# Moving squares, products and state scans between four engines in layer 0 of a two-layer streaming encoder

## The chip, the cores and the metric

The kernel runs on one core of a Trainium2 chip. The core has five engines that follow instruction streams of their own: TensorE (PE in the profile, with its weight loads as PEld), VectorE (DVE), ScalarE (ACT), GpSimd (POOL) and SyncE (SP, which here issues the transfers). They meet at semaphores only: an instruction that waits holds up all that stands behind it on its engine. The metric is the device time of one execution in microseconds, lower is better.

## What is computed

Two groups of frames, 1024 of a prompt and 8 x 16 of running streams, 1152 columns in all, go through two trunk layers with the same weights. Layer 0, in which the change lies, cut to what matters:

```python
h = rmsnorm(x, norm_mix[0])                       # x * rsqrt(mean(x*x)) * w
proj = h @ w_in                                   # 1024 -> S5 input u, q, k, v, z, b, a
# mixer A: S5, 32 groups of 16 channels, a complex state of 64 for each
lam_bar = exp(lam * dt)
b_bar = ((lam_bar - 1) / lam)[..., None] * b      # operators, from the weights alone
x_t = lam_bar * x_{t-1} + b_bar @ u_t             # a scan along time
y_t = real(c @ x_t) + d * u_t
# mixer B: gated DeltaNet, 4 heads
q, k = l2norm(silu(conv(q))) * 128**-0.5, l2norm(silu(conv(k)))
# ... chunked delta rule with a triangular inverse per chunk ...
x = x + concat(a_out, b_out) @ w_out_ab
x = x + swiglu(rmsnorm(x, norm_ffn[0]))
```

Layer 1 has windowed attention in place of the mixers; a last norm ends it.

## The kernel before

Activations lie transposed, features over the 128 partitions and the 1152 columns along them, in three blocks `b` of 384 (`BW`). Every large product is made of fp32r matmuls from two-part operands (high and low part, three matmuls for each piece of 128 rows): `gemm_block` with L320 to L322, 24 matmuls for a block of one panel of 128 output columns. Its result lies in a PSUM bank of the pool `pg`, of which there are two; the matmuls of a block can't begin before the block two back has been read out by VectorE ("evicted"). A panel of weights comes by DMA into `raw`, ScalarE makes the high part (L297, `whi`), VectorE the low part (L298, `wlo`).

Up to about 360 us, layer 0 has these stages, in the order of the program:

- The first norm. For each block ScalarE makes eight squares (L992), GpSimd adds them in pairs (L994), and `rms` sums the four that are left over the partitions by plain fp32 matmuls with a matrix of ones (L370). The two first panels follow for that block.
- `s5_coefs`, a generator that is advanced between the other stages. Its first part makes the exponentials, a sine (L1702, ScalarE) and the powers of `lam_bar` as long chains of small instructions on GpSimd (L1670 to L1754). Its second makes the S5 operators in four rounds `m`: products of 128x128 (`B1p`, `B`, `t`) and of 128x1024 and 128x1152 (`every`, L1744: `lb`, `tl`, `cl`, `tc`), sums of two of them (L1783, L1794), transposes and small matmuls on TensorE (`plb` L1788, `pkt` L1800), and DMAs of the results.
- Beside it TensorE makes the S5 input in panels 1 to 3, evicted by L970 (`ut`, three times for each panel), and one panel of gates, evicted by L1036.
- Matmuls `pe` (L1078) apply the operators, ScalarE copies the results into `XE`, and the S5 states are scanned in `XE`: 15 steps inside chunks of 16 (L1093 to L1095, four instructions of 256 elements each step), 8 steps over the chunks (L1099 to L1101), and 7 corrections (two products of 512 elements, L1105, then two sums by VectorE, L1106 and L1107).
- For each of four DeltaNet heads, the key and query panels go through `conv_in` (evicted by L1128 to L1131, four taps of 128x1176 on VectorE, L1138 and L1140), `conv_silu`, and `l2norms`: squares (L1158, GpSimd), a sum over the partitions on TensorE (`sums`, L333), logarithm and exponential on ScalarE, a product on VectorE (L1163). The chunk matrices follow (`pS`, `pQ`, `pK`, `pB`, L1178 to L1206).

Nobody wrote the order by hand: the program is emitted with priorities (`Sooner` raises them), and the framework's scheduler, which plans with a timeline of its own, lays down each engine's list. On the chip each list runs as it stands.

Of the kernel before, what the change touches and what calls it, by code (L numbers as in the profile page):

```python
# [18 lines left out]
AF = mybir.ActivationFunctionType  # L19
ALU = mybir.AluOpType  # L20
# [182 lines left out]
def body(tc, nc, I, O):  # L203
# [7 lines left out]
    V, S, P, PE, Q = nc.vector, nc.scalar, nc.gpsimd, nc.tensor, nc.sync  # L211
# [150 lines left out]
    def rms(r, b, parts, first=0, banks=None):  # L362


        s = blk(b)
        y, v = r[:, s], ssq[:, s]
        t = rp.tile([128, BW], F32, name="nt", tag="nt", bufs=1)
        p = mbank("pn")[:, :BW]
        for i, sq in enumerate(parts):
            PE.matmul(p, onesf, sq, start=(i == 0), stop=(i == len(parts) - 1))  # L370
        tables = [tc.keep_in_program_order(log_tables())] if b == first else []
        act = [behind(S.activation(y, p, AF.Ln, scale=1.0 / D, bias=epsc), *tables)]
        V.tensor_scalar(v, p, 1.0 / D, EPS, op0=ALU.mult, op1=ALU.add)
        act.append(S.activation(y, y, AF.Exp, scale=-0.5))
        V.scalar_tensor_tensor(t, y, -0.5, v, ALU.mult, ALU.mult)
        V.tensor_mul(t, t, y)
        o = y
        if banks is not None:
            o = banks[b] = p
        V.scalar_tensor_tensor(o, t, 1.5, y, ALU.add, ALU.mult)  # L380
        return act
# [538 lines left out]
    L8 = L0.tile([128, 2, 2, 16], F32, name="L8")  # L920
# [58 lines left out]
    h, r = operand(slots("h")), new_r()  # L979
    ut, ev_uu = ev_u()  # L980
    ln = []
    room = itertools.cycle((None, None, "pS", "pQ", None, "pB"))
    for b in range(NB):
        q = [n0.tile([128, BW], F32, name="sq0", tag="sq0", bufs=KC) for k in range(KC)]
        for k in range(KC):
            wk = nw[:, k:k + 1]
            if k % 2:
                S.activation(h[b][k][0], x[:, k, blk(b)], AF.Copy, scale=wk)
            else:
                V.tensor_scalar(h[b][k][0], x[:, k, blk(b)], wk, None, op0=ALU.mult)  # L990
            V.scalar_tensor_tensor(h[b][k][1], x[:, k, blk(b)], wk, h[b][k][0], ALU.mult, ALU.subtract)
            S.activation(q[k], x[:, k, blk(b)], AF.Square)  # L992
            if k % 2:
                P.tensor_add(q[k], q[k], q[k - 1])  # L994
        ln += rms(r, b, q[1::2])
        for w, ev in zip(W, (ev_ba, ev_uu)):
            tag = next(room)
            gemm_block(w, h, b, ev, p=tag and mbank(tag))
# [12 lines left out]
    ln = [behind(S.activation(t1[q4, :], t1[q4, :], AF.Exp, scale=-1.0), tables)]  # L1011
# [40 lines left out]
    PW = L2.tile([128, 2, 16, 2, 16], F32, name="PW")  # L1052
    FE = L2.tile([128, 9, 2, 16], F32, name="FE")
# [26 lines left out]
    for k in range(2):  # L1080
        cur = XE[:, TP // CS + k::2]
        prev = x0e if k == 0 else XE[:, TP // CS:TP // CS + 2 * NS - 1:2]
        for q in range(2):
            t = e6.tile([128, NS, 2, 16], F32, name="cst", tag="cst", bufs=1)
# [3 lines left out]
    XG = XE[:, 0:TP // CS].rearrange("p (a c) q g -> p a c q g", c=16)  # L1088
    sc = ssq.rearrange("p (u v g) -> p u v g", v=2, g=16)
    for c in range(1, 16):  # L1090
        t = sc[:, 0:16].rearrange("p (a k) q g -> p a k q g", k=2)
        for k in range(2):
            P.tensor_tensor(t[:, :, k], L8[:, k][:, None].to_broadcast([128, 8, 2, 16]), XG[:, :, c - 1], ALU.mult)  # L1093
        P.tensor_tensor(XG[:, :, c], XG[:, :, c], t[:, :, 0], ALU.add)
        P.tensor_tensor(XG[:, :, c], XG[:, :, c], t[:, :, 1, ::-1, :], ALU.add)  # L1095
    P.memset(FE[:, 0], 0.0)
    for a in range(8):
        t = sc[:, 0:2]
        P.tensor_tensor(t, PW[:, :, 15], FE[:, a][:, None].to_broadcast([128, 2, 2, 16]), ALU.mult)  # L1099
        P.tensor_tensor(FE[:, a + 1], XG[:, a, 15], t[:, 0], ALU.add)  # L1100
        P.tensor_tensor(FE[:, a + 1], FE[:, a + 1], t[:, 1, ::-1, :], ALU.add)  # L1101
    for a in range(1, 8):
        t = sc[:, 2:34].rearrange("p (k c) q g -> p k c q g", k=2)
        for k in range(2):
            P.tensor_tensor(t[:, k], PW[:, k], FE[:, a][:, None].to_broadcast([128, 16, 2, 16]), ALU.mult)  # L1105
        V.tensor_tensor(XG[:, a], XG[:, a], t[:, 0], ALU.add)  # L1106
        V.tensor_tensor(XG[:, a], XG[:, a], t[:, 1, :, ::-1, :], ALU.add)  # L1107
    Q.dma_start(O["s5p"], XE[:, TP // CS - 1])
# [42 lines left out]
    def l2norms(ys, tables):  # L1151

        act = []
        for y, rr, f in ys:
            for b in range(NB):
                s = blk(b)
                sq = cv.tile([128, BW], F32, name="sq", tag="sq", bufs=2)
                P.tensor_mul(sq, y[:, s], y[:, s])  # L1158
                act.append(behind(S.activation(rr[:, s], sums(sq, BW), AF.Ln, bias=epsc), tables))
        for y, rr, f in ys:  # L1160
            act.append(S.activation(rr[:, :T], rr[:, :T], AF.Exp, scale=-0.5, bias=f))
            for b in range(NB):
                V.tensor_mul(y[:, blk(b)], y[:, blk(b)], rr[:, blk(b)])  # L1163
        return act
# [4 lines left out]
    for hh in range(H):  # L1169
# [4 lines left out]
        ln = l2norms([(kk, ak, 0.0), (qq, aq, lq)], tables)  # L1174
        for b in range(NB):
            s = blk(b)
            pS, pQ, pB, pK = mbank("pS"), mbank("pQ"), mbank("pB"), mbank("pK")
            PE.matmul(pB[:, :BW], sel[:, hh, :], RHL[:, s], start=True, stop=True)  # L1178
            for t in range(3):
                c = blk(3 * b + t, 128)  # L1180
# [235 lines left out]
    with Sooner(1500):  # L1416
        t = NT - 1
# [20 lines left out]
        for h0 in (0, 2):  # L1438
# [20 lines left out]
            for q in range(4):  # L1459
# [4 lines left out]
                for i in range(2):  # L1464
                    for e in range(2):
                        b = 2 * q + e
# [145 lines left out]
    h, r = nxt["h"], nxt["r"]  # L1612
# [37 lines left out]
def s5_coefs(env):  # L1650

    nc, cf, I, sgn, ident, mbank = (env[n] for n in ("nc", "c5", "I", "sgn", "ident", "mbank"))
    d_T, d_lb, d_cl, L8 = (env[n] for n in ("d_T", "d_lb", "d_cl", "L8"))
# [84 lines left out]
    def g16(v):  # L1738
        return v[:, :, None].to_broadcast([128, 8, 16])

    def every(eng, o, z, v):

        s = list(o.shape)
        eng.tensor_mul(o, z.rearrange("p j g -> p g j")[:, :, :, None].to_broadcast(s), v[:, :, None, :].to_broadcast(s))  # L1744
# [17 lines left out]
    for m in range(4):  # L1762
        gs = slice(8 * m, 8 * m + 8)

        def rot(n, shape, dt=F32):
            return cf.tile([128] + list(shape), dt, name=n, tag=n, bufs=1)

        B1p, B2, t2, t3 = (rot(n, (8, 16)) for n in ("B1p", "B2", "t2", "t3"))
        B, C = (t[:, :, m].rearrange("p k (g c) -> p k g c", c=16) for t in (Ball, Call))
        B1 = B1p  # L1770
        V.tensor_mul(B1, g16(fr[:, gs]), B[:, 0])
        P.tensor_mul(t2, g16(fi[:, gs]), B[:, 1])
        V.tensor_add(B1, B1, t2)
        V.tensor_mul(B2, g16(fr[:, gs]), B[:, 1])
        P.tensor_mul(t3, g16(fi[:, gs]), B[:, 0])
        V.tensor_sub(B2, B2, t3)

        V.tensor_scalar(C[:, 0], C[:, 0], sgn, -1.0, op0=ALU.mult, op1=ALU.mult)
        V.tensor_scalar(C[:, 1], C[:, 1], -1.0, None, op0=ALU.mult)
        lb, tl = (cf.tile([128, 8, CS, 16], F32, name=n, tag=n, bufs=1) for n in ("lb", "tl"))  # L1780
        every(V, lb, PR[:, CS - 1::-1, gs], B1)
        every(P, tl, PIs[:, ::-1, gs], B2)
        V.tensor_add(lb, lb, tl)  # L1783
        lt = cf.tile([128, 8, 128], F32, name="lt", tag="lt", bufs=1)
        for g0 in (0, 4):
            p = mbank("plb", "pS" if g0 else "pQ")
            for g in range(4):
                PE.transpose(p[:, g * 128:g * 128 + 128], lb[:, g0 + g].rearrange("p j c -> p (j c)"), ident)  # L1788
            S.copy(lt[:, g0:g0 + 4], p.rearrange("p (g i) -> p g i", g=4))
        Q.dma_start(d_lb[m].rearrange("p (g i) -> p g i", g=8), lt)  # L1790
        cl, tl = (cf.tile([128, 8, CS + 1, 16], F32, name=n, tag=n, bufs=1) for n in ("cl", "tc"))
        every(V, cl, PR[:, :, gs], C[:, 0])
        every(P, tl, PI[:, :, gs], C[:, 1])
        V.tensor_add(cl, cl, tl)  # L1794
        Q.dma_start(d_cl[m].rearrange("p (g i) -> p g i", g=8), cl[:, :, 1:, :].rearrange("p g e c -> p g (e c)"))
        kt = cf.tile([16, 8, 128], F32, name="kt", tag="kt", bufs=1)
        for g0 in (0, 4):
            p = mbank("pkt", "pB" if g0 else "pK")
            for g in range(4):
                PE.matmul(p[0:16, g * 128:g * 128 + 128], B1p[:, g0 + g], cl[:, g0 + g, 0:CS, :].rearrange("p e c -> p (e c)"), start=True, stop=True)  # L1800
            S.copy(kt[:, g0:g0 + 4], p[0:16].rearrange("p (g i) -> p g i", g=4))
        t4 = cf.tile([16, 8, 16], F32, name="t4", tag="t4", bufs=1)
        P.tensor_tensor(t4, ident[0:16, 0:16][:, None, :].to_broadcast([16, 8, 16]), sD[:, gs][:, :, None].to_broadcast([16, 8, 16]), ALU.mult)
        P.tensor_add(kt[:, :, 0:16], kt[:, :, 0:16], t4)
        for j in range(CS):
            Q.dma_start(d_T[gs, 16 * j:16 * j + 16, 16 * j:].rearrange("g c i -> c g i"), kt[:, :, 0:128 - 16 * j])
# [206 lines left out]
```

## Time and profile before

| | |
|---|---|
| three timed runs | 2709.35, 2709.62, 2715.86 us; median 2709.62 |
| the profiled execution | 2709.62 us, of which its span is 2707.8 us |
| granted TensorE clock, mean | 0.973 of full speed |
| busy share: PE, DVE, ACT, POOL | 94%, 73%, 42%, 60% |

The span runs from the first instruction to the last. "Busy" counts an instruction from its start to its end, so an instruction that is held up while it runs counts as busy too. The shares are means over stages that have little in common, so the stages are read apart below.

### The profile page before, as it was taken

Reading aid. Unit: us, or ns where it says so; the run is one execution under the profiler, and the core shown is the slowest. Engines: PE = TensorE matmul, PEld = TensorE weight load, DVE = VectorE, ACT = ScalarE, POOL = GpSimd, SP = SyncE. Lnnn points to the kernel's source line nnn. Section 1 sums busy time; section 2 is a strip of 40 time slices with the busy share of each in tenths; the row PEclk is TensorE's granted clock in tenths of the full one; section 3 lists DMA queues with packets and bytes.
Section 4 is the critical chain, followed back from the end, with each engine's and each line's share of the span. In section 5 each row is a group of like instructions: output and inputs, shape, how many; then the busy total and the mean of one; then the engine's idle time right before and its main releaser. Section 6 shows DMA issues by size and latency. Waiting matters only on the chain.

```text
span 2707.8 us, 40377 instructions
## 1 busy us (share of the span) xinstructions
PE 2556.9 (94%) x14777; PEld 2382.5 (88%) x14777; DVE 1979.3 (73%) x3235; ACT 1146.3 (42%) x2312; POOL 1625.4 (60%) x1659
## 2 busy tenths in 40 slices
PE   6898899999799999989999999999889999989996
PEld 5787798999799999989998977677889999989996
DVE  7847874567878777798866245555878777788967
ACT  5234465345544444443333134434544444444333
POOL 8749532125698888887532022213589888888735
PEclk9899999999999999999999999998999999999998
DMA  6432377633122222253213200202122222243311
GB/s 208 126 114 77 102 237 230 190 121 111 37 101 79 91 74 74 93 185 100 93 38 106 69 16 19 93 30 86 43 98 82 86 76 74 76 177 119 96 49 70
DMA packets 164166, 267.21 MB, mean 99 GB/s; under 512 B 34188, under 2 KB 123948, under 8 KB 162928
## 3 DMA queue, kind: packets, MB, share of 16 engines
q1 hardware_dynamic: 163392, 262.28, 29.9%
q8 instruction: 116, 1.90, 0.3%
q10 hardware_dynamic: 576, 2.36, 0.2%
q14 instruction: 82, 0.67, 0.1%
HBM read 186.92 MB, written 79.51 MB: 98 GB/s over the span
## 4 chain that ended last, share of the span: by engine, by line
PE 68%; POOL 11%; DVE 11%; DMA 4%; issue 4%; ACT 1%; SPq 1%; DVEq 0%; POOLq 0%; ACTq 0%
PE pa L455 7%; PE pa L454 7%; PE pa L453 7%; PE pd L455 3%; PE pd L453 3%; PE pd L454 3%; PE b L453 3%; PE b L455 3%; PE b L454 3%; PE pg L320 3%; PE pg L322 3%; PE pg L321 3%; PE pO L1923 2%; PE pg L1543 2%; PE pg L1544 2%
## 5 line engine op out<-in xcount | busy, mean ns | idle before, releaser
L453 PE MATMUL pa<-u,whi 128*128 128x384 f32 x904 | 307.4, 341 | 20.6 <-ACT whi L535 10.9
L454 PE MATMUL pa<-u,whi 128*128 128x384 f32 x904 | 306.3, 339 | 1.1 <-DVE u L269 1.1
L455 PE MATMUL pa<-u,wlo 128*128 128x384 f32 x904 | 298.1, 338 | 6.3 <-DVE wlo L536 6.3
L535 ACT CAST whi<-x 128x1024 fp32r<-128x1024 f32 (+2 forms) x184 | 132.5, 747 | 257.1 <-PE pa L454 172.1
L454 PE MATMUL pd<-g,whi 128*128 128x384 f32 x708 | 240.2, 339 | 0.0
L453 PE MATMUL pd<-g,whi 128*128 128x384 f32 x708 | 239.3, 338 | 0.0
L455 PE MATMUL pd<-g,wlo 128*128 128x384 f32 x708 | 237.8, 338 | 0.4 <-DVE wlo L298 0.4
L536 DVE TENSOR_TENSOR wlo<-x,whi 128x1024 fp32r<-128x1024 f32 (+2 forms) x184 | 213.0, 1180 | 24.7 <-ACT whi L535 24.4
L1884 POOL TENSOR_SCALAR p<-p,rd 128x192 f32<-128x192 f32 (+3 forms) x80 | 60.0, 752 | 278.4 <-DVE rd L1878 157.3
L453 PEld LDWEIGHTS pa<-u,whi 128*128 128x128 f32 x904 | 171.5, 190 | 25.5 <-ACT whi L535 14.5
L297 ACT CAST whi<-raw 128x1024 fp32r<-128x1024 f32 x113 | 116.6, 1049 | 173.7 <-PE pg L321 81.6
L531 POOL TENSOR_TENSOR x<-x 128x256 f32<-128x256 f32 (+1 forms) x186 | 169.4, 931 | 24.9 <-DVE wlo L536 18.8
L531 POOL TENSOR_TENSOR x<-raw 128x256 f32<-128x256 f32 (+1 forms) x186 | 169.4, 933 | 21.5 <-DVE wlo L536 13.3
L298 DVE TENSOR_TENSOR wlo<-raw,whi 128x1024 fp32r<-128x1024 f32 x113 | 165.3, 1465 | 22.7 <-ACT whi L297 20.3
L455 PEld LDWEIGHTS pa<-u,wlo 128*128 128x128 f32 x904 | 170.8, 190 | 7.7 <-DVE wlo L536 7.6
L531 POOL TENSOR_TENSOR cm<-raw 128x256 f32<-128x256 f32 (+1 forms) x150 | 144.3, 983 | 49.8 <-DVE wlo L536 18.5
L454 PEld LDWEIGHTS pa<-u,whi 128*128 128x128 f32 x904 | 171.8, 190 | 2.3 <-DVE u L269 1.9
L453 PE MATMUL pa<-u,x 128*128 128x384 f32 x428 | 145.8, 341 | 5.3 <-ACT x L535 2.8
L320 PE MATMUL pg<-h0h,whi 128*128 128x384 f32 x384 | 135.4, 353 | 12.1 <-DVE ut L970 11.4
L454 PE MATMUL pa<-u,x 128*128 128x384 f32 x428 | 144.9, 338 | 0.0
L455 PE MATMUL pa<-u,x 128*128 128x384 f32 x428 | 141.6, 339 | 0.0
L790 DVE TENSOR_TENSOR g<-gf,g 128x384 fp32r<-128x384 f32 x132 | 137.4, 1066 | 5.3 <-ACT g L789 5.3
(735 smaller groups left out, 8113.7 us busy)
## 6 DMA issues: line engine op xcount, KB each, us to landing
gf<-d_g SPq DMA_DIRECT2D x44, 576.0 KB
raw<-in_wd_dram SPq DMA_DIRECT2D x44, 512.0 KB
raw<-in_wg_dram SPq DMA_DIRECT2D x24, 512.0 KB
raw<-in_wu_dram SPq DMA_DIRECT2D x24, 512.0 KB
raw<-in_win_dram SPq DMA_DIRECT2D x21, 512.0 KB
x<-in_wg_dram SPq DMA_DIRECT2D x20, 512.0 KB
x<-in_wu_dram SPq DMA_DIRECT2D x20, 512.0 KB
d_r<-x SPq DMA_DIRECT2D x24, 384.0 KB
```

Source lines behind the costliest of these rows:

```text
L297: S.copy(hi, raw)
L298: V.tensor_sub(lo, raw, hi)
L320: PE.matmul(p[:, :BW], hi[:, c], rh, start=(i == 0), stop=False)
L321: PE.matmul(p[:, :BW], hi[:, c], rl, start=False, stop=False)
L322: PE.matmul(p[:, :BW], lo[:, c], rh, start=False, stop=(i == len(ks) - 1))
L453: PE.matmul(p, hi[:, c], uh, start=start, stop=False, skip_group_check=more)
L454: PE.matmul(p, hi[:, c], ul, start=False, stop=False, skip_group_check=more)
L455: PE.matmul(p, lo[:, c], uh, start=False, stop=stop, skip_group_check=more)
L531: (P.tensor_add if sg > 0 else P.tensor_sub)(cm[:, 256 * j:256 * (j + n)], fa, ga)
L535: S.copy(hi[:, c], src)
L536: V.tensor_sub(lo[:, c], src, hi[:, c])
L790: eng.tensor_sub(op[1], t, op[0])
```

## The change

Five edits, all in layer 0. The eight squares of the first norm go to TensorE as they are, without GpSimd's sums in pairs. In the operators, the second product of each pair (`t2`, `t3`, `tl`, `tc`) is made by VectorE. All products and sums of the state scans are VectorE's too. The squares of keys and queries are made by ScalarE.

```diff
@@ first norm
-            if k % 2:
-                P.tensor_add(q[k], q[k], q[k - 1])
-        ln += rms(r, b, q[1::2])
+        ln += rms(r, b, q)
@@ state scans
         for k in range(2):
-            P.tensor_tensor(t[:, :, k], L8[:, k][:, None].to_broadcast([128, 8, 2, 16]), XG[:, :, c - 1], ALU.mult)
-        P.tensor_tensor(XG[:, :, c], XG[:, :, c], t[:, :, 0], ALU.add)
-        P.tensor_tensor(XG[:, :, c], XG[:, :, c], t[:, :, 1, ::-1, :], ALU.add)
+            V.tensor_tensor(t[:, :, k], L8[:, k][:, None].to_broadcast([128, 8, 2, 16]), XG[:, :, c - 1], ALU.mult)
+        V.tensor_tensor(XG[:, :, c], XG[:, :, c], t[:, :, 0], ALU.add)
+        V.tensor_tensor(XG[:, :, c], XG[:, :, c], t[:, :, 1, ::-1, :], ALU.add)
...
-        P.tensor_tensor(t, PW[:, :, 15], FE[:, a][:, None].to_broadcast([128, 2, 2, 16]), ALU.mult)
-        P.tensor_tensor(FE[:, a + 1], XG[:, a, 15], t[:, 0], ALU.add)
-        P.tensor_tensor(FE[:, a + 1], FE[:, a + 1], t[:, 1, ::-1, :], ALU.add)
+        V.tensor_tensor(t, PW[:, :, 15], FE[:, a][:, None].to_broadcast([128, 2, 2, 16]), ALU.mult)
+        V.tensor_tensor(FE[:, a + 1], XG[:, a, 15], t[:, 0], ALU.add)
+        V.tensor_tensor(FE[:, a + 1], FE[:, a + 1], t[:, 1, ::-1, :], ALU.add)
...
-            P.tensor_tensor(t[:, k], PW[:, k], FE[:, a][:, None].to_broadcast([128, 16, 2, 16]), ALU.mult)
+            V.tensor_tensor(t[:, k], PW[:, k], FE[:, a][:, None].to_broadcast([128, 16, 2, 16]), ALU.mult)
@@ squares of keys and queries
-                P.tensor_mul(sq, y[:, s], y[:, s])
+                S.activation(sq, y[:, s], AF.Square)
@@ S5 operators, in each of four rounds
-        P.tensor_mul(t2, g16(fi[:, gs]), B[:, 1])
+        V.tensor_mul(t2, g16(fi[:, gs]), B[:, 1])
...
-        P.tensor_mul(t3, g16(fi[:, gs]), B[:, 0])
+        V.tensor_mul(t3, g16(fi[:, gs]), B[:, 0])
...
-        every(P, tl, PIs[:, ::-1, gs], B2)
+        every(V, tl, PIs[:, ::-1, gs], B2)
...
-        every(P, tl, PI[:, :, gs], C[:, 1])
+        every(V, tl, PI[:, :, gs], C[:, 1])
```

The scheduler makes its lists anew. Up to the end of layer 0's mixers all five differ; behind that only a few rows change their places. Line numbers behind L993 are lower by two in the changed kernel. Three places follow.

TensorE at the start of the program, as a difference: the sum over the squares `sq` of block 0, before the first panel's matmuls `pg`.

```order
+L370 MATMUL pn<-sq_276,onesf 128x384
 L370 MATMUL pn<-sq_277,onesf 128x384
+L370 MATMUL pn<-sq_278,onesf 128x384
 L370 MATMUL pn<-sq_279,onesf 128x384
+L370 MATMUL pn<-sq_280,onesf 128x384
 L370 MATMUL pn<-sq_281,onesf 128x384
+L370 MATMUL pn<-sq_282,onesf 128x384
 L370 MATMUL pn<-sq_283,onesf 128x384
```

Four fp32 matmuls have become eight, and so in each of the three blocks.

VectorE before, in the operators' first round, from the eviction of the last block of the first S5 panel (`ut<-pB`) to that of the next block (`ut<-pg`); `XE` with 4 rows is scratch of the DeltaNet gates.

```order
L970 TENSOR_TENSOR ut<-pB,r 128x48x8
L1773 TENSOR_TENSOR B1p<-B1p,t_1045 128x128
L298 TENSOR_TENSOR wlo<-raw,whi 128x1024
L1776 TENSOR_TENSOR B_1044<-B_1044,t_1046 128x128
L1013 SCALAR_TENSOR_TENSOR XE<-XE 4x1152
L1744 TENSOR_TENSOR lb<-c_582,B1p 128x1024
L1744 TENSOR_TENSOR cl<-c_582,C 128x1152
L970 TENSOR_TENSOR ut<-pg,r 128x48x8
```

The same place in the changed kernel:

```order
L970 TENSOR_TENSOR ut<-pB,r 128x48x8
L1771 TENSOR_TENSOR B1p<-B1p,t_1045 128x128
L1774 TENSOR_TENSOR B_1044<-B_1044,t_1046 128x128
L1770 TENSOR_TENSOR t_1106<-c_611,B 128x128
L1773 TENSOR_TENSOR t_1107<-c_611,B 128x128
L1742 TENSOR_TENSOR lb<-c_582,B1p 128x1024
L1742 TENSOR_TENSOR cl<-c_582,C 128x1152
L298 TENSOR_TENSOR wlo<-raw,whi 128x1024
L1742 TENSOR_TENSOR tc<-c_583,C 128x1152
L1011 SCALAR_TENSOR_TENSOR XE<-XE 4x1152
L970 TENSOR_TENSOR ut<-pg,r 128x48x8
```

The eviction now has ten instructions between it and the last one, in place of six; two products `t` and the large product `tc`, GpSimd's before, stand among them.

VectorE before, in the first head, from the product with the norm of the keys (`cy`) over the next panel's taps (`ca`) to the chunk matrices (`A`):

```order
L1163 TENSOR_TENSOR cy<-cy,ca 128x384 x3
L1138 TENSOR_SCALAR ca<-cr,cw 128x1176
L1140 SCALAR_TENSOR_TENSOR ca<-cr,cw,ca 128x1176 x3
L1195 SCALAR_TENSOR_TENSOR A<-pS,CT,Dm 128x128 x3
L1128 TENSOR_TENSOR cr<-pg,r 128x384
```

The same place in the changed kernel:

```order
L1161 TENSOR_TENSOR cy<-cy,ca 128x384 x3
L1093 TENSOR_TENSOR XE<-XE,ssq 128x8x32
L1136 TENSOR_SCALAR ca<-cr,cw 128x1176
L1091 TENSOR_TENSOR ssq<-L_98,XE 128x8x32 x2
L1138 SCALAR_TENSOR_TENSOR ca<-cr,cw,ca 128x1176
L1092 TENSOR_TENSOR XE<-XE,ssq 128x8x32
L1138 SCALAR_TENSOR_TENSOR ca<-cr,cw,ca 128x1176
L1093 TENSOR_TENSOR XE<-XE,ssq 128x8x32
L1193 SCALAR_TENSOR_TENSOR A<-pS,CT,Dm 128x128 x3
```

The steps of the scan (L1091 to L1093 here) stand one by one among the taps and ahead of `A`.

## Rows read from the trace of the kernel before

**Rows 1.** Windows: length, busy (count) of PE, PEld, DVE, ACT, POOL; clock; DMA
```profile
48.00:143.00 95.00, 72.53 (x401) 67.05 (x401) 66.25 (x58) 28.99 (x45) 67.16 (x101) 0.86 0.48 139
143.00:360.00 217.00, 199.74 (x1162) 179.22 (x1162) 156.52 (x253) 95.52 (x185) 133.94 (x168) 0.97 0.30 93
```

**Rows 2.** What TensorE waited for, 40 to 130 us: total, times, longest
```profile
PE pg L320 <- DVE ut L970: 11.4, 2, 10.2
```

**Rows 3.** A window of TensorE work without a wait, columns as in rows 1
```profile
127.00:142.00 15.00, 15.00 (x89) 15.00 (x88) 3.20 (x4) 3.39 (x5) 0.45 (x1) 1.00 0.88 279
```

**Rows 4.** TensorE by form, 47.9 to 142.9 us: count, busy us, mean ns, idle before
```profile
L1800 PE MATMUL pkt<-cl,B1p 128*16 128x128 f32 x64 | 9.4, 310 | 5.9 <-DVE cl L1794 5.9
L1788 PE MATMUL plb<-ident,lb 128*128 128x128 f32 x32 | 5.1, 313 | 4.9 <-DVE lb L1783 4.8
```

**Rows 5.** The operators' stage as one window, columns as in rows 1
```profile
56.00:124.00 68.00, 45.82 (x245) 41.54 (x244) 59.91 (x51) 15.44 (x30) 59.44 (x74) 0.80 0.40 109
```

**Rows 6.** VectorE by form, 40 to 125 us, columns as in rows 4
```profile
L1744 DVE TENSOR_TENSOR cl<-c,C 128x1152 f32<-128x1152 f32 x4 | 9.1, 2280 | 0.6 <-DMA d_cl<-cl 0.6
L1776 DVE TENSOR_TENSOR B<-B,t 128x128 f32<-128x128 f32 x4 | 5.4, 1348 | 0.0
L1774 DVE TENSOR_TENSOR B<-c,B 128x128 f32<-128x128 f32 x4 | 4.4, 1111 | 0.0
L1771 DVE TENSOR_TENSOR B1p<-c,B 128x128 f32<-128x128 f32 x4 | 4.3, 1070 | 6.1 <-POOL c L1731 6.0
```

**Rows 7.** The large products, line L1744, columns as in rows 10
```profile
L1744 DVE TENSOR_TENSOR lb<-c,B1p x4: 1226/1532/1931, 63.8 to 117.6; 128x1024 f32<-128x1024 f32 x4
L1744 DVE TENSOR_TENSOR cl<-c,C x4: 1344/2288/3201, 65.0 to 119.4; 128x1152 f32<-128x1152 f32 x4
```

**Rows 8.** VectorE in time, 40 to 130 us: two instructions of the operators' stage
```profile
56.06 0.32 DVE L1771 TENSOR_TENSOR B1p<-c,B 128x128 f32<-128x128 f32 x1 [6.04 <-POOL c L1731]
...
105.35 4.13 DVE L1776 TENSOR_TENSOR B<-B,t 128x128 f32<-128x128 f32 x1
```

**Rows 9.** GpSimd in time, 104 to 115 us: beside the last of rows 8
```profile
106.42 2.24 POOL L1744 TENSOR_TENSOR tc<-c,C 128x1152 f32<-128x1152 f32 x1
108.63 0.70 POOL L1061 TENSOR_TENSOR ssq<-PW 128x256 f32<-128x256 f32 x1
109.29 0.76 POOL L1060 TENSOR_TENSOR PW<-PW 128x256 f32<-128x256 f32 x1
```

**Rows 10.** GpSimd's sums of squares: ns least, median, most; first and last start
```profile
L994 POOL TENSOR_TENSOR sq<-sq,sq x12: 998/1172/1411, 6.1 to 37.7; 128x384 f32<-128x384 f32 x12
```

**Rows 11.** The chain that ended last, 1440 to 1460 us: fp32 sums, two records a matmul
```profile
1454.62 1.94 PE pn L370 x6
```

**Rows 12.** ScalarE in time, 39 to 48 us: the sine's table and the sine
```profile
40.84 1.28 ACT L1702 ACT_TABLE_LOAD   x1
46.64 0.35 ACT L1702 ACTIVATE c<-c 128x32 f32<-128x32 f32 x2 [4.51 <-POOL c L1700]
```

**Rows 13.** TensorE in time, at the start of the operators' use
```profile
142.94 1.25 PE L1078 MATMUL pe<-U,LB 128*64 128x144 f32 x16
```

**Rows 14.** What TensorE waited for, 130 to 360 us
```profile
PE pn L333 <- POOL sq L1158: 10.0, 5, 5.5
```

**Rows 15.** ScalarE's squares in the first norm, columns as in rows 10
```profile
L992 ACT ACTIVATE sq<-x x24: 507/510/531, 4.6 to 30.5; 128x384 f32<-128x384 f32 x24
```

**Rows 16.** The time of the scans as one window, columns as in rows 1
```profile
176.00:300.00 124.00, 109.46 (x571) 96.38 (x570) 97.04 (x147) 51.88 (x98) 117.89 (x138) 0.94 0.25 75
```

**Rows 17.** Lines L1163, L1085 and L1106 on VectorE, columns as in rows 10
```profile
L1163 DVE TENSOR_TENSOR cy<-cy,ca x24: 545/586/1180, 202.9 to 342.6; 128x384 f32<-128x384 f32 x24
L1085 DVE TENSOR_TENSOR cst<-x0e,L x2: 419/630/841, 144.2 to 177.0; 128x256 f32<-128x256 f32 x2
L1106 DVE TENSOR_TENSOR XE<-XE,ssq x7: 693/1252/1767, 258.9 to 296.4; 128x512 f32<-128x512 f32 x7
```

**Rows 18.** VectorE by form, 176 to 300 us, columns as in rows 4
```profile
L1163 DVE TENSOR_TENSOR cy<-cy,ca 128x384 f32<-128x384 f32 x15 | 11.9, 847 | 0.0
```

## The prediction

> **What bounds the kernel now.** I read the windows by stage first, then TensorE's waits in each, then the lists of the engines that it waited for. In the profiled execution the span is 2707.8 us and 1.8 us lie outside it; its time, 2709.62, is also the median of the three runs, so the sum below can be made against it. TensorE carries the kernel (94% busy), so a change is worth what it gives back of TensorE's idle time, and of its lower clock, in the stages that it touches. There are two such stages [rows 1]. From 48 to 143 us (operators) TensorE was busy for 72.5 of 95 us at a granted clock of 0.86. From 143 to 360 us (states and heads) it was busy for 199.7 of 217, so 17 us were idle, at 0.97.
>
> TensorE's longest wait in the first was for VectorE's eviction `ut`: 11.4 us, 10.2 of it at once [rows 2]. What did that stage need? A stretch without a wait had 89 panel matmuls in 15.00 us, 0.17 each [rows 3]. The stage has 401 matmul records, 96 of which are the small ones of the operators (9.4 + 5.1 = 14.5 us) [rows 1, 4]. So 305 x 0.17 + 14.5 = 66 us were needed of the 95, and 29 us were lost. Besides `ut`, 5.9 and 4.8 us were waits for `cl` and `lb` [rows 4], sums that VectorE makes from GpSimd's products. The other 7 lie in the clock of 0.86, which stretched the busy part.
>
> VectorE was busy for 59.9 of the 68 us in which it made the operators, and GpSimd for 59.4 [rows 5]. Both were slower than they need be: the same form on VectorE took 1.34 us at the least and 2.28 in the mean [rows 6, 7], the 128x128 sum L1776 took 4.13 us once [rows 8], while GpSimd went through three instructions of 2.24, 0.70 and 0.76 us [rows 9]. Its neighbour L1771, a 128x128 product, took 0.32 [rows 8].
>
> **First norm, 0 to 48 us.** Twelve sums of about 1.17 us leave GpSimd, 14 us [rows 10]. TensorE gets twelve fp32 matmuls more. Three such took 1.94 us [rows 11], so it is 12 x 0.65 = 7.8 us. Most of that fills waiting for squares and weights at the start; I leave +1 us in the sum, bounds 0 and +8. The effect is on what follows. The sine waited 4.51 us for GpSimd [rows 12], whose chain of small instructions stood behind the sums: nine of them, 10.6 us, by the changed list. Now ScalarE itself is last: its table for the sine was loaded by 40.84 + 1.28 = 42.1 [rows 12]; with up to 1 us for the longer sum of block 2 and 0.35 for the sine it ends at about 43.5 instead of 47.0. The powers on GpSimd follow it, and the first product of the operators, which waited 6.04 us for them and began at 56.06 [rows 8]. That moves earlier by 3.5 us if the sine's shift alone carries through, by 10.6 if all the time of the sums does. I take 9.6, near the top, since in the changed list no sum stands any more among the powers: 46.5.
>
> **Operators, 48 to 143 us.** VectorE takes over, in each of four rounds, two products of 0.32 [rows 8], one of 128x1024 at 1.23 and one of 128x1152 at 1.34 [rows 7], the least of their kinds, 12.8 us in all. It loses stretch where GpSimd has no large product any more: for `cl` 4 x (2.28 - 1.34) = 3.8 us, for L1776, L1774 and L1771 4 x (1.35 - 0.32), 4 x (1.11 - 0.32) and 4 x (1.07 - 0.32) = 10.3, so 14 [rows 6, 7, 8]. So VectorE's sum stays at about 59: 59.9 - 14 + 12.8. From 46.5, with 3 us of waits for the powers, that ends at 108 in place of 124. GpSimd still has the powers `PW` to make beside it, 24 instructions by its list, at most some 0.7 us each [rows 9], so 17 us. At worst each holds VectorE up for its whole length; at best none does. I take 5, nearer to the low end, because the products that made the long overlaps are gone: 112 in place of 124. Behind the last of it TensorE still has about 81 panel matmuls and some transposes ahead of the first `pe` by the changed list, 0.17 each with a little more, so `pe` stands at about 128 in place of 142.94 [rows 13]. And that list has 23 panel matmuls (4 us) more ahead of `pe` than before, work that is done by then instead of later: 15 + 4 = 19 us gained. Bounds: 7, if the mutual holding stays as it is and only the earlier start and the shorter waits remain; 26, if there is none and nearly all of the 29 lost us come back.
>
> On the mutual holding the Trainium skill (SBUF — State Buffer, section SBUF: two separate sides) says that VectorE and GpSimd share a port pair which is locked for a whole instruction, and that the other one then blocks. The trace agrees where a 0.32-us form took 4.13 us beside 3.7 us of GpSimd's work [rows 8, 9]. By that rule alone all of GpSimd's remaining work would add to VectorE's, which is the low end of 7 us; by the rows, stretch is partial, and I keep 19.
>
> **States and heads, 143 to 360 us.** The squares of keys and queries leave GpSimd, and with them a wait of 10.0 us (`pn` for `sq`) [rows 14]. ScalarE makes one in 0.51 us [rows 15], 24 in 12 us; it was busy for 51.9 of 124 us [rows 16] and has room. Against this stand the scans. From 176 to 300 us VectorE was busy for 97.0 of 124 us and GpSimd for 117.9 [rows 16]. VectorE gets 60 instructions of 256 elements, 0.42 each by L1085's least, 14 of 512 at 0.69 by L1106's least [rows 17], and 24 of 64 elements, which the trace lacks: between nothing and the 0.42 of 256 elements I take 0.2. That is 25 + 10 + 5 = 40 us. What comes back is stretch: the product L1163 took 0.847 in the mean of this window [rows 18] and 0.545 at the least [rows 17]. If all of VectorE's work there was stretched like that, its 97 us were 62 at rest; if only that line was, they were 92. So VectorE would have 102 to 132 us of work in these 124; nearer the middle, 118. It becomes nearly full, and the scan's steps stand in its list among taps and ahead of `A`, so that evictions and chunk matrices come later. My walk through both lists puts TensorE's waits for VectorE at 15 to 22 us. Before, 17 us were idle [rows 1], and the clock of 0.94 in the scans' window [rows 16] cost some more. I take -2 us, bounds -15 and +10 for the middle of the work range, and more if VectorE's work comes out at its top (rival 1). The scan's result is needed only near 360 us, so its own length costs nothing.
>
> The rows behind 360 us are nearly the same; I put nothing there, within 5 us either way.
>
> **The sum.** 2709.6 + 1 - 19 - 2 = 2690 us. Its own range, from -26 to -7 for the operators with the other terms near their values, is 2680 to 2701.
>
> **Rivals.** 1, slower: VectorE becomes the bound of the heads. The 74 larger scan instructions and the 24 small ones then cost the stretched price, since GpSimd isn't empty and VectorE's own taps stand between them: L1085 took 0.84 and L1106 1.77 at the most [rows 17], so 60 x 0.84 + 14 x 1.25 + 24 x 0.4 = 77 us in place of 40. With 92 us of the rest, VectorE has 169 us in 124: 45 late, of which the operators give back 19: 2709.6 + 45 - 19 = 2735. It turns the sum's sign when the 98 instructions together come out 25 us dearer than I took them, 0.26 us each. For it: VectorE's list is one queue, and the evictions stand in it. Against it: it needs both GpSimd's stretch and the top of the rest, and the stretch should fall as GpSimd empties.
>
> 2, no change: the operators gain only their low end, 7 us (VectorE and GpSimd go on holding each other up, over the powers in place of the products), and the heads give 0: 2709.6 + 1 - 7 + 0 = about 2703, within 0.3% of before. For it: the 17 us of powers lie in the same time as VectorE's products. Against it: the longest instruction beside the stretched sum was a product of 128x1152 [rows 9], which goes. By the rule of the Trainium skill (SBUF — State Buffer, section SBUF: two separate sides) it would go this way, and the traces bear that out as far as 0.18.
>
> 3, more: no hold in the operators (-26), the wait for `sq` gone for good and VectorE keeping up in the heads (-15): 2709.6 - 41 = 2668. For it: VectorE at rest needs only 102 us of 124 by the low bound. Against it: the order, with scan steps ahead of `A`.
>
> **Chances.** The forecast 0.55, rival 1 0.12, rival 2 0.18, rival 3 0.15. 0.3% of the time is 8.1 us, which is about what a measurement of this kernel can tell from no change. Faster by more than that, below 2701.5: the forecast, rival 3 and a small part of rival 2, 0.72. Within: most of rival 2, 0.16. Slower: rival 1, 0.12. The range of 8 in 10 reaches to rival 3's time and a little over half way to rival 1's: 2668 to 2716. The likeliest case alone has 2680 to 2701.
>
> **What would show it right or wrong.** First norm: the sine without a wait for GpSimd, its end near 43.5, L1769 (L1771 before) at about 46.5 us. Operators: the wait for `ut` of 10.2 us gone or below 4, L1774 near 0.32 us in the median, VectorE's large products at 1.2 to 1.5, the first `pe` at 127 to 130 us with TensorE's clock near 1 from 60 us on. Heads: no wait of `pn` for `sq`; the scan instructions (L1091 to L1093) at 0.42 us, VectorE's busy time in the window of the scans 110 to 125 of 124; TensorE waiting for VectorE's `A`, `cr` and taps 15 to 22 us in place of `sq`. Wrong it would be if the scan instructions took 0.7 us or more (rival 1), if 128x128 sums still took over 1 us in the mean (rival 2), or if a new wait of TensorE came up that I have put at nothing: for ScalarE, behind the squares, or for the twelve sums over the partitions at the start.

## The result and the profile after

The changed kernel took 2678.35 us (median, 2677.58 to 2681.24), against 2710.52 for the kernel before beside it: 0.9877 of it, 95% interval 0.9861 to 0.9893, or 32 us. Forecast was 20, with a range that held the time; 2678.35 lies 2 us below the likeliest case's own range. A second timing of the changed kernel gave 0.9873 (0.9858 to 0.9888).

The windows of the changed kernel, columns as in [rows 1]:

```profile
48.00:143.00 95.00, 83.99 (x510) 78.16 (x510) 68.33 (x89) 31.51 (x50) 36.75 (x57) 0.95 0.56 165
143.00:360.00 217.00, 208.87 (x1237) 193.13 (x1237) 177.11 (x385) 116.38 (x222) 28.19 (x87) 0.98 0.39 117
```

In the same 95 us TensorE got through 510 matmul records in place of 401, and in the next 217 us through 1237 in place of 1162 [rows 1]. GpSimd's busy time fell from 67 to 37 and from 134 to 28 us. Both stages gained, the second far more than I had put down.

TensorE's waits from 40 to 130 us, in the order of [rows 2]:

```profile
PE pg L320 <- DVE XE L963: 5.5, 1, 5.5
PE pct L1026 <- ACT RT L1019: 3.8, 1, 3.8
PE pg L320 <- DVE ut L970: 1.6, 2, 0.9
```

The wait of 10.2 us for the eviction `ut` is gone, those for `lb` and `cl` too (nine instructions, not ten, stand between the two evictions of the changed list shown above). New are 5.5 us for VectorE's `XE` and 3.8 us for ScalarE's `RT`, which is made from `XE`. From 130 to 360 us, in the order of [rows 14]:

```profile
PE pg L320 <- DVE cr L1126: 3.9, 2, 3.7
PE pS L1179 <- DVE A L1193: 1.7, 1, 1.7
PE pK L1181 <- ACT AQ L1195: 1.5, 2, 1.1
PE pQ L1180 <- DVE AQ L1196: 0.7, 1, 0.7
```

The row left out is 0.3 us for a transfer. No wait for squares is left, and 6.3 us of waits for VectorE, where I had put 15 to 22. The prices of single instructions on VectorE (least, median, most in ns; first and last start):

```profile
L1091 DVE TENSOR_TENSOR ssq<-L,XE x30: 409/418/439, 167.0 to 225.1; 128x256 f32<-128x256 f32 x30
L1097 DVE TENSOR_TENSOR ssq<-PW,FE x8: 205/218/226, 226.4 to 272.9; 128x64 f32<-128x64 f32 x8
L1103 DVE TENSOR_TENSOR ssq<-PW,FE x14: 675/683/687, 227.3 to 276.5; 128x512 f32<-128x512 f32 x14
L1161 DVE TENSOR_TENSOR cy<-cy,ca x24: 545/551/558, 195.1 to 314.7; 128x384 f32<-128x384 f32 x24
L1774 DVE TENSOR_TENSOR B<-B,t x4: 268/305/666, 58.3 to 104.2; 128x128 f32<-128x128 f32 x4
L1742 DVE TENSOR_TENSOR cl<-c,C x4: 1352/1470/2246, 60.2 to 109.1; 128x1152 f32<-128x1152 f32 x4
L1781 DVE TENSOR_TENSOR lb<-lb,tl x4: 1206/1209/1219, 70.7 to 114.9; 128x1024 f32<-128x1024 f32 x4
```

The scan's steps cost what was forecast, 0.42, 0.22 and 0.68 us, and nearly without spread. L1161 (L1163 before) is back at its least, 0.55, in place of 0.847 in the mean [rows 18]. The 124 us in which the scans run, as a window:

```profile
160.00:284.00 124.00, 116.38 (x662) 105.64 (x657) 116.25 (x263) 67.41 (x134) 11.20 (x24) 0.97 0.26 80
```

VectorE is busy for 116.25 of 124 us (118 forecast), GpSimd for 11. The longest idle time of VectorE in that window, by form, is a wait for TensorE:

```profile
L1128 DVE TENSOR_TENSOR cr<-pg,r 128x256 f32<-128x256 f32 x7 | 2.9, 416 | 5.5 <-PE pg L322 5.5
```

So, full as it is, VectorE still waited for TensorE there.

To compare programs whose lists differ, I gave each TensorE record the usual distance of its line from the next matmul (0.17 us for a panel's) and looked when a run had reached the sum that the kernel before had reached at a given time. The twelve added sums are left out. The lead in us, worked out so, for all kernels of the study (the last column is the difference of the profiled spans); two profiles of the changed kernel differ in it by 1.6 to 1.9 us. Three profiled executions lie 6 us or more from the median of their kernel: `u_sq` (squares on GpSimd) 8 us above it, `v_cl2` (two cl) 9 and `a_ops` (products alone moved) 6 below; their last column is off by about as much.

| kernel | lead at 143 | at 360 | at 680 | at 1675 | at the end |
|---|---|---|---|---|---|
| changed | 14.5 | 29.4 | 23.6 | 19.7 | 30.9 |
| changed, again | 12.8 | 27.7 | 25.2 | 21.3 | 29.0 |
| changed, scans on GpSimd | 13.8 | 14.2 | 11.1 | 6.2 | 14.3 |
| changed, squares on GpSimd | 13.3 | 26.3 | 27.8 | 21.8 | 20.5 |
| changed, products on GpSimd | 1.9 | 22.1 | 16.2 | 13.5 | 22.3 |
| changed, sums on GpSimd | 8.4 | 23.6 | 15.8 | 11.0 | 15.4 |
| before, scans alone moved | -0.4 | 14.6 | 16.2 | 10.5 | 14.9 |
| before, products alone moved | 8.3 | 10.5 | 17.7 | 16.0 | 26.0 |
| changed, loads first | 13.3 | 24.1 | 26.8 | 23.0 | 32.1 |
| the same, kt on VectorE | 21.9 | 29.4 | 23.7 | 22.0 | 32.7 |
| the same, two cl | 17.4 | 32.6 | 31.6 | 25.3 | 34.0 |
| the same, both | 17.5 | 32.7 | 32.2 | 26.2 | 34.6 |

So the 31 us of the profiled spans are 14.5 in the operators, 15 in the heads, -10 from there to layer 1's attention, and +11 in that attention (1675 to 1950 us) and behind it.

**The step that missed its time.** The first product of the operators began at 56.56 us, as before, and not at 46.5. ScalarE in time:

```profile
42.85 0.35 ACT L1700 ACTIVATE c<-c 128x32 f32<-128x32 f32 x2
```

GpSimd in time, the factor that the first product reads:

```profile
46.64 0.25 POOL L1729 TENSOR_TENSOR c<-c,c 128x32 f32<-128x32 f32 x1
```

VectorE in time:

```profile
50.48 0.57 DVE L1776 TENSOR_SCALAR C<-C,pc 128x128 f32<-128x128 f32 x1 [8.25 <-DMA C<-in_sC_dram]
...
53.96 0.55 DVE L963 TENSOR_TENSOR XE<-pg,r 36x384 f32<-36x384 f32 x1
...
56.56 0.29 DVE L1769 TENSOR_TENSOR B1p<-c,B 128x128 f32<-128x128 f32 x1
```

And SyncE's transfers in time:

```profile
39.92 0.39 SPq L1756 DMA_DIRECT2D d_T<-c  x1
40.35 5.47 SPq L1759 DMA_DIRECT2D C<-in_sC_dram  x1
```

The sine and the factor were there when I had said, 43.2 and 46.9 us. But VectorE stood for 8.25 us on the load of `C`, ahead in its list, and behind it TensorE for `XE`. The load was issued at 40.35, behind the transfer of zeros to `d_T`, which waits for a memset of GpSimd (L1755, at 39.68 us). In the kernel before SyncE had the two the other way round:

```profile
29.21 0.42 SPq L1761 DMA_DIRECT2D C<-in_sC_dram  x1
40.09 0.39 SPq L1758 DMA_DIRECT2D d_T<-c  x1
```

The scheduler had moved one load behind one waiting transfer, and I hadn't read that list.

### The profile page after: what moved, and what is told of

It is laid out like the page before. It is cut to its first block, busy times and chain, and to the rows that moved or that the text cites. A ratio compares the mean times of both kernels' runs of the same rounds, so it can differ in the third digit from the quotient of the medians.

```text
span 2676.9 us, 40367 instructions
## 1 busy us (share of the span) xinstructions
PE 2553.2 (95%) x14801; PEld 2379.2 (89%) x14801; DVE 1971.1 (74%) x3349; ACT 1157.9 (43%) x2338; POOL 1474.5 (55%) x1509
## 4 chain that ended last, share of the span: by engine, by line
PE 64%; DVE 9%; POOL 6%; issue 2%; DMA 2%; ACT 1%; DVEq 0%; POOLq 0%; SPq 0%; ACTq 0%
PE pa L455 7%; PE pa L453 7%; PE pa L454 7%; PE pd L455 4%; PE pd L453 3%; PE pd L454 3%; PE b L455 3%; PE b L453 3%; PE b L454 3%; PE pO L1921 2%; PE pg L320 2%; PE pg L322 2%; PE pg L321 2%; PE pg L1541 2%; PE pg L1542 2%
## 5 line engine op out<-in xcount | busy, mean ns | idle before, releaser
L453 PE MATMUL pa<-u,whi 128*128 128x384 f32 x904 | 306.9, 340 | 16.2 <-DVE bt L568 9.7
L531 POOL TENSOR_TENSOR x<-x 128x256 f32<-128x256 f32 (+1 forms) x186 | 171.2, 942 | 25.2 <-DVE wlo L536 18.7
L455 PEld LDWEIGHTS pa<-u,wlo 128*128 128x128 f32 x904 | 171.0, 190 | 11.2 <-DVE wlo L536 11.1
L531 POOL TENSOR_TENSOR x<-raw 128x256 f32<-128x256 f32 (+1 forms) x186 | 169.2, 932 | 20.6 <-DVE wlo L536 12.1
```

Of the source, the lines that this page charges most:

```text
L453: PE.matmul(p, hi[:, c], uh, start=start, stop=False, skip_group_check=more)
L455: PE.matmul(p, lo[:, c], uh, start=False, stop=stop, skip_group_check=more)
L531: (P.tensor_add if sg > 0 else P.tensor_sub)(cm[:, 256 * j:256 * (j + n)], fa, ga)
```

## The experiments

**The scans back on GpSimd** (`u_scan`).

```diff
-            V.tensor_tensor(t[:, :, k], L8[:, k]..., XG[:, :, c - 1], ALU.mult)
+            P.tensor_tensor(t[:, :, k], L8[:, k]..., XG[:, :, c - 1], ALU.mult)
...
```

> The changed kernel with the state scans back on GpSimd; the other edits stay. Theory: the heads gained because both the scans and the squares left GpSimd; with the scans there VectorE is stretched again (the product L1161 at 0.7 to 0.85 us in the mean of the scans' window, 0.55 without), and of the 14 us that the stage from 143 to 360 gained, half goes: 2683 to 2690. Rival: the squares alone made the gain (TensorE waits for no squares on GpSimd any more), and the 40 us of scans on VectorE, which then is busy for 116 of 124 us, cost: this kernel is as fast or faster, 2668 to 2678.

It took 2694.87 us, 0.9932 (0.9911 to 0.9953) of before. The loss is larger than the theory's 5 to 12 us, and the heads lose all of their gain: lead 13.8 at 143 us, 14.2 at 360. TensorE's waits from 130 to 340 us, then a scan line on GpSimd, two forms on VectorE, and the scans' window:

```profile
PE pS L1179 <- DVE A L1193: 7.0, 2, 5.8
PE pg L320 <- DVE cr L1126: 6.4, 1, 6.4
PE pS L1179 <- DVE cy L1161: 2.2, 1, 2.2
PE pQ L1180 <- DVE cy L1161: 0.8, 1, 0.8
PE pQ L1180 <- DVE AQ L1196: 0.6, 1, 0.6
```
```profile
L1091 POOL TENSOR_TENSOR ssq<-L,XE x30: 726/772/1884, 167.4 to 226.8; 128x256 f32<-128x256 f32 x30
```
```profile
L1161 DVE TENSOR_TENSOR cy<-cy,ca 128x384 f32<-128x384 f32 x12 | 9.1, 809 | 3.6 <-ACT ca L1159 3.6
L1104 DVE TENSOR_TENSOR XE<-XE,ssq 128x512 f32<-128x512 f32 x7 | 8.5, 1221 | 11.7 <-POOL FE L1098 10.4 <-POOL ssq L1103 1.3
```
```profile
162.00:286.00 124.00, 107.05 (x569) 96.47 (x569) 93.12 (x143) 55.51 (x110) 96.52 (x120) 0.92 0.24 72
```

With the scans on GpSimd VectorE has 93 us to do in place of 116, and TensorE waits longer for it (17.0 us in place of 6.3). Its product takes 0.81 us again, and, what I had not counted, VectorE stands for 11.7 us ahead of L1104, the first of its own sums in the scan's corrections, 10.4 of them because GpSimd's steps over the chunks aren't ready; taps, evictions and chunk matrices wait behind that in the list. The rival (the squares made the gain) is out.

**The scans alone moved** (`a_scan`), the kernel before with that one edit.

> The kernel before with the state scans alone on VectorE; squares, operators and the first norm stay. Theory: GpSimd empty of the scans is what the heads gained from (squares then wait for nothing, VectorE runs unstretched): the stage from 143 to 360 us gains 10 to 15 us by itself, time 0.994 to 0.996 of before. Rival: the gain needs the squares on ScalarE too, or the operators' gain ahead of it: the wait of pn for sq stays above 5 us and the time is within 0.3% of before.

2693.87 us, 0.994 (0.992 to 0.9959); lead 14.6 us at 360 us, all of it won in the heads. The wait for the squares on GpSimd fell from 10.0 us [rows 14] to 3.1, though no edit touches the squares, and the stage got 91 records more than the 1162 before:

```profile
PE pn L333 <- POOL sq L1158: 3.1, 1, 3.1
```
```profile
143.00:360.00 217.00, 210.21 (x1253) 192.97 (x1252) 180.21 (x366) 103.90 (x194) 59.94 (x78) 0.98 0.34 104
```

**The squares back on GpSimd** (`u_sq`).

> The changed kernel with the squares of keys and queries back on GpSimd; the other edits stay. Theory: GpSimd is nearly empty without the scans, so the squares wait for nothing there; TensorE waits 0 to 3 us for them, each is slower than on ScalarE, and the time is 2678 to 2683. Rival: the squares made the gain of the heads: the wait of pn for sq is back with 8 to 12 us, and the time is 2686 to 2694.

2681.35 us, 0.9885 (0.9865 to 0.9906): no difference from the changed kernel that could be told. One wait of 2.2 us for a square came:

```profile
PE pn L333 <- POOL sq L1156: 2.2, 1, 2.2
```

The move of the squares, for which I had booked the end of a wait of 10 us, is worth 1 to 3 us by 360 us. What made them late was the queue of scans ahead of them.

**The products back on GpSimd** (`u_ops`), and **the products alone moved** (`a_ops`).

```diff
-        V.tensor_mul(t2, g16(fi[:, gs]), B[:, 1])
+        P.tensor_mul(t2, g16(fi[:, gs]), B[:, 1])
...
-        every(V, tl, PI[:, :, gs], C[:, 1])
+        every(P, tl, PI[:, :, gs], C[:, 1])
```

> The changed kernel with the second products of the operators back on GpSimd; the other edits stay. Theory: VectorE and GpSimd hold each other up again (128x128 products and sums of VectorE at 1 us in the mean, the large ones at 2), the stage from 48 to 143 us loses most of the 15 us that it gained, and the time is 2688 to 2695. Rival: the wait for C decides when the operators end, and the products cost little on either engine: 2676 to 2683.

> The kernel before with the operators' second products alone on VectorE. Theory: the operators' stage gains 8 to 14 us by itself, as its loss was when the products were taken back (12.6 us by 143 us); the heads give back part, since the scans are still GpSimd's: time 0.995 to 0.998 of before. Rival: it needs the earlier start that the first norm's edit gives: the last large sum of the operators at 118 us or later (122.5 before), within 0.2% of before.

`u_ops`: 2686.32 us, 0.99 (0.9879 to 0.992), between the two expectations. The lead at 143 us fell from 14.5 to 1.9, as the theory has it, but the heads won 20 us in place of 15, so the whole loss was 8 us. Of its waits from 40 to 130 us two are back, for the large sums `lb` and `cl`, and `lb` takes 2.25 us in the median, 4.60 at the most, where the changed kernel has 1.21:

```profile
PE plb L1786 <- DVE lb L1781: 8.2, 3, 4.3
PE pkt L1798 <- DVE cl L1792: 4.8, 2, 3.4
```
```profile
L1781 DVE TENSOR_TENSOR lb<-lb,tl x4: 1220/2252/4596, 74.8 to 117.9; 128x1024 f32<-128x1024 f32 x4
```

`a_ops`: 2690.18 us, 0.9923 (0.9903 to 0.9942), lead 8.3 at 143 us and 10.5 at 360. By 143 us this lies in the theory's 8 to 14; the time came out lower than the range. In the profiled execution, the fastest of its four, the program won 15 us more behind 360 us (item 6 below).

**The sums back on GpSimd** (`u_adds`).

```diff
+            if k % 2:
+                P.tensor_add(q[k], q[k], q[k - 1])
-        ln += rms(r, b, q)
+        ln += rms(r, b, q[1::2])
```

> The changed kernel with the sums in pairs of the first norm back on GpSimd, and so four matmuls for each block's sum. Theory: the first norm's edit is worth little, since VectorE's operators don't begin earlier with it (56.6 us against 56.1): the time is 2676 to 2682, and the operators' first product stands at 55 to 58 us. Rival: it is what clears GpSimd's list ahead of the powers: without it the first product comes at 60 us or later, the first pe 4 us or more later, and the time is 2683 to 2689.

2690.41 us, 0.9931 (0.991 to 0.9952). The theory failed: 6 us of the operators' lead go (8.4 in place of 14.5). The rival is near the time and has the first `pe` right (138.7 us, 6 later), but not the mechanism, since the first product comes at the same time (56.1 us). What comes later are the large products (`lb`: 61.8 to 119.4 us in place of 59.0 to 112.0) and, by the last sum, the end of the operators, 122.4 us against 114.9:

```profile
L1783 DVE TENSOR_TENSOR lb<-lb,tl x4: 1211/1241/1476, 73.4 to 122.4; 128x1024 f32<-128x1024 f32 x4
```

The other half of the 12 us that this kernel loses lies behind 360 us (item 6 below). Sums and products help each other: the products alone bring 8.3, the sums alone 1.9 (`u_ops`), both 14.5.

**The loads first** (`loads_first`), to test the wait for `C`. TensorE's list stays the same.

```diff
-    zt = sm((128, 128))
-    P.memset(zt, 0.0)
-    Q.dma_start(d_T..., zt...)
     Ball, Call = ...
     Q.dma_start(Ball, I["sB"]...)
     Q.dma_start(Call, I["sC"]...)
+    zt = sm((128, 128))
+    P.memset(zt, 0.0)
+    Q.dma_start(d_T..., zt...)
```

> The changed kernel with one edit: the loads of the S5 operands (B, C) are written ahead of the zeros for d_T, so that SyncE issues them first. Theory: in the changed kernel the load of C waits on SyncE behind the transfer of the zeros, which waits for GpSimd's memset, and VectorE sits 8.2 us for C at 42 us; without that the first product of the operators (56.6 us now) starts at 47 to 48, the first large product (59.0) at 53.5 to 55, when the powers are there, TensorE's wait of 5.5 us for XE goes, and the time falls by 4 to 7 us, to 2671 to 2675. Rival: VectorE's sum of work up to 112 us decides, and GpSimd's powers hold what starts earlier: the first product earlier, but the first pe within 2 us of 132.6 and the time within 3 us of 2678.

2682.13 us (2677.53 to 2684.99), 0.9888 (0.9867 to 0.9909): no difference from the changed kernel that could be told. The theory's gain failed, and the rival is only near: the time lies 4 us from its 2678 and the first `pe`, at 136.6 us, 4 us behind the changed kernel's. The place of the wait was right, its price was not. VectorE in time:

```profile
48.58 0.33 DVE L1769 TENSOR_TENSOR B1p<-c,B 128x128 f32<-128x128 f32 x1 [1.20 <-POOL c L1729]
...
97.66 1.36 DVE L1742 TENSOR_TENSOR cl<-c,C 128x1152 f32<-128x1152 f32 x1 [5.95 <-DMA d_cl<-cl]
```

SyncE in time:

```profile
85.24 3.68 SPq L1804 DMA_DIRECT2D d_T<-kt  x8
...
91.32 0.57 SPq L1793 DMA_DIRECT2D d_cl<-cl  x1
```

The 8 us won at the start of the stage went into the next waits: 6 us of VectorE for the one buffer of `cl`, whose transfer stood on SyncE behind those of `kt`, and TensorE waited 12.1 us for `ut`, four times, where it had waited 1.6. VectorE's part of the stage as a window from its first product to its last sum, in the changed kernel and then here:

```profile
56.50:116.20 59.70, 54.34 (x317) 51.04 (x317) 58.04 (x70) 20.55 (x34) 27.82 (x34) 0.94 0.53 139
```
```profile
48.50:117.30 68.80, 56.69 (x323) 53.20 (x323) 59.56 (x69) 20.83 (x34) 44.89 (x57) 0.90 0.40 106
```

The same work, 58 and 60 us: in the changed kernel it runs nearly without a gap, and what starts earlier has 9 us of gaps.

**A way out of that** (`v_kt`, `v_cl2`, and `v_both`).

```diff
-        P.tensor_add(kt[:, :, 0:16], kt[:, :, 0:16], t4)
+        V.tensor_add(kt[:, :, 0:16], kt[:, :, 0:16], t4)
...
-    cl, tl = (cf.tile(..., bufs=1) for n in ("cl", "tc"))
+    cl, tl = (cf.tile(..., bufs=2 if n == "cl" else 1) for n in ("cl", "tc"))
```

> loads_first with one small sum more on VectorE (kt, 16x128, four times), whose result SyncE sends to d_T ahead of other transfers. Theory: in loads_first GpSimd reached this sum only behind the powers, SyncE waited with the transfers of kt at 85 us for it, d_cl stood behind them, and VectorE waited 6.0 us for d_cl at 97 us, which ate the time that the earlier load of C had brought. With the sum on VectorE that wait goes, the last large sum of the operators (116.0 us) comes at 109 to 111, the first pe 4 to 6 us earlier, and the time is 2671 to 2675 on the scale on which the changed kernel has 2678. Rival: another engine is late next (TensorE's waits for ut stay at 10 us or more): within 3 us of 2678.

> loads_first with two buffers for cl in place of one, so that VectorE's next product need not wait for the transfer of the last. Theory: the wait of 6.0 us goes here too, with the transfers still late on SyncE: the last large sum at 109 to 111 us, but LB comes by the same queue, so the first pe gains 0 to 4 us and the time is 2674 to 2678 on the scale of 2678. Rival: the wait only moves, from the buffer of cl to that of kt or lt: no change of the last large sum (115 to 117 us).

> The changed kernel itself once more, as the scale for the next kernel on the same chip: 0.986 to 0.990 of before.

> The changed kernel with the loads of B and C ahead of the zeros, kt's sum on VectorE and two buffers for cl. Theory: VectorE then waits neither for C nor for d_cl; with both the last large sum of the operators comes at 108 to 111 us, and by 360 us the kernel is 3 to 6 us ahead of the changed one; its time is 0.997 to 0.999 of the changed kernel's. Rival: what is won by 143 us is lost in the heads again, where VectorE has 116 us of work in 124: no difference beyond 0.1%.

The times: `v_kt` 2678.96 us, 0.989 (0.9859 to 0.9921); `v_cl2` 2684.74, 0.9902 (0.9871 to 0.9934), with runs from 2675.6 to 2688.67; `v_both` 2674.94, 0.9872 (0.9851 to 0.9892), beside the changed kernel's 0.9873. None differs from the changed kernel by more than its interval. So no theory's time came. `v_kt` and `v_both` have that of their rivals; `v_cl2` lies 7 us above its theory's, but its rival is out as well, since the last large sum moved. By the profiles the first `pe` came at 129.0 to 129.1 us in all three (132.6 changed, 136.6 with the loads first), and the last large sum at 111.1, 111.7 and 113.0 (114.9 changed). `v_cl2` and `v_both` are 3 us further at 360 us, `v_kt` is 7 further at 143 and no further at 360. TensorE's wait for `ut` stays in all three, with 5.5 to 9.0 us (1.6 changed); in `v_both`, from 40 to 130 us:

```profile
PE pg L320 <- DVE ut L970: 9.0, 2, 7.3
```

## Why the prediction was right, and where it was off

The sign and the two places were right, and the sum was short by 12 us: 2690 predicted, 2678 measured. The range held the time because it reached down to rival 3's.

1. First norm, +1 us: at 48 us the changed kernel is 0.5 us behind, worked out as in the table (2.2 in its second profile). Right. TensorE's longest wait there is now for ScalarE's squares, 5.1 us; for GpSimd's sums it was 10.8 in all.
2. The first product "at about 46.5 us": wrong, 56.56. The part of the chain that I had followed came on time; the load of `C` on a queue that I had not followed did not. With it moved, the product came at 48.6, and the stage still ended no earlier. So the early start was never worth what I had booked for it.
3. The operators, -19: 12.8 to 14.5. VectorE's sum was right, 58 us for 59. But it began ten microseconds later than forecast and had almost none of the 3 us of waits and 5 of holding that I had added, so that it ended at 116 us for 112 (by the terms as they stand 46.5 + 58.7 + 3 + 5 is 113), and the first `pe` came at 132.6 for 128. Two errors in opposite senses left a size near the truth, which is luck. Rival 2, in which the two engines go on holding each other up, is out: L1774 took 0.305 us in the median and 0.67 at the most, and VectorE did its 58 us of work with GpSimd busy for 27.8 us beside it. `a_ops`, `u_ops` and `u_adds` show that the products make it, and that GpSimd's lighter list ahead of them helps.
4. States and heads, -2: this is the term that was mis-sized; it measured -15. Its prices were right (0.42, 0.22, 0.68 us, VectorE 116 us busy). What failed is the step from a nearly full VectorE to "TensorE's waits for VectorE at 15 to 22 us": they were 6.3. I hadn't read what they were before. All waits of the kernel before from 130 to 360 us, beside the 10.0 us for squares [rows 14]:

```profile
PE pQ L1182 <- DVE AQ L1198: 3.8, 3, 2.4
PE pS L1181 <- DVE cy L1163: 1.5, 1, 1.5
PE pB L1178 <- ACT AQ L1192: 1.2, 1, 1.2
PE pg L320 <- DVE cr L1128: 0.4, 1, 0.4
PE pS L1181 <- DVE A L1195: 0.3, 1, 0.3
```

So TensorE waited for VectorE for 6.0 us already, and 40 us of scans more on VectorE left that as it was, while the wait for squares went. TensorE's idle time in the 217 us fell from 17 to 8 us, and the clock in the scans' window rose from 0.94 to 0.97, which is worth some 4 us (an estimate, 0.03 x 124); together that is most of the 15. I charged VectorE's added work against TensorE and left out that the scan on GpSimd had held VectorE's list up too: for 5.8 us ahead of its own sums L1106 and L1107 in the kernel before, for 11.7 ahead of one line in `u_scan`. How much of the gain is that waiting and how much the stretch of VectorE's instructions no run separates. Rival 1 (slower) needed scan steps at 0.7 us or more; the most that L1091 took was 0.439. Rival 3 named the mechanism of this stage, VectorE keeping up, and its -15 is what the stage gave.
5. The squares: I took the wait of 10.0 us for them as theirs. `a_scan` and `u_sq` show that it was the scans' queue on GpSimd: with the scans gone and the squares in their old place it is 3.1 or 2.2 us.
6. Behind 360 us, 0: the sum is 1.5 us gained, of 10 lost and 11 won, and both go with TensorE's granted clock. At the lower of its two levels, 1.2 GHz, panel matmuls follow each other every 0.32 us in place of 0.17 (at 57 and at 61 us of the changed kernel), so that a microsecond at that level loses about half of one. In the changed kernel the clock fell at 378 and 412 us, each time right behind 2.0 us in which TensorE was idle. By the clock rows of the traces TensorE was at that level for 38 us in the kernel before from 360 to 1675 us, and for 58 us in the same work of the changed kernel: some 10 us lost. From 1675 to 1950 us it was 31 us, and 10 in the changed kernel: some 10 us won. Parts of these as windows of the same work, the kernel before and then the changed one, first from 360 us and then from 1675 us on:

```profile
360.00:680.00 320.00, 306.87 (x2320) 288.79 (x2319) 201.54 (x387) 169.41 (x291) 103.46 (x139) 0.97 0.57 178
```
```profile
330.70:656.50 325.80, 313.16 (x2320) 294.67 (x2319) 194.77 (x379) 168.83 (x286) 104.14 (x135) 0.95 0.57 176
```
```profile
1675.00:1950.00 275.00, 261.52 (x1337) 197.72 (x1335) 173.84 (x451) 124.67 (x382) 87.76 (x91) 0.94 0.18 62
```
```profile
1655.40:1919.60 264.20, 251.79 (x1336) 189.53 (x1334) 172.23 (x450) 125.17 (x382) 88.00 (x90) 0.98 0.20 65
```

For the other kernels of the table half the difference in time at 1.2 GHz gives the lead's change in both stretches to within 4 us, with one exception (`a_ops`, 5.4 us won from 360 to 1675 us without such a difference). What makes the clock fall in one kernel and not in another is open. I had taken TensorE's list as nearly the same, but of its last 6400 rows some 340 differ, in layer 1's attention. That list alone doesn't decide it: eight other kernels of the study have the changed kernel's list there by line and tile, and in the stretch from 1675 to 1950 us they were at 1.2 GHz for 10 us (`loads_first`, `v_kt`) to 27 us (`u_adds`); the changed kernel's second profile has 17, and so has `a_scan` with another list.

On GpSimd's price: the Trainium skill (GPSIMD Engine Reference, section 4.1, Engine selection) says that GpSimd is about twice as slow as VectorE in operations with two inputs. The runs agree: 0.772 against 0.418 us for L1091, 1.432 against 0.683 for L1103 (medians, `u_scan` and the changed kernel; by the least of each it is 1.8 and 1.9 times).

## What to carry to other kernels

Where VectorE and GpSimd alternate in one chain, both can pay, as in `u_scan`: price what VectorE waits for GpSimd's half, and not only what its own work grows by. A wait for one engine's result may be the queue of other work ahead of it on that engine; ask what happens to it when only that queue is moved. When a scheduler makes the lists anew, read every queue that a moved stage depends on, SyncE's loads too, and compare the granted clock in stages that the edit doesn't touch: here it took 10 us and gave 10 back.

## What was not expected of the hardware

VectorE, busy for 116 of the scans' 124 us, kept TensorE waiting for 6.3 us from 130 to 360 us; busy for 93 of 124 (`u_scan`), it kept TensorE waiting for 17.0 us: its share of busy time told nothing of who waits for it. And behind 360 us, where no edit lies, the lead of a kernel goes up and down by some 10 us with the time that TensorE spends at 1.2 GHz; with one and the same list of TensorE that time was 10 us in one kernel and 27 in another.
